# Recurrent heads: the keys and queries of a head in three tiles of memory, one for each chunk of tokens, in place of one

## The chip, the cores and the metric

The kernel runs on one core of a Trainium2 chip, in one launch. The metric is the device time of one execution in microseconds (us). The core's engines are TensorE (PE in the profile: matrix products; PEld are its weight loads, which run beside the products), VectorE (DVE), ScalarE (ACT), GpSimd (POOL) and SyncE (SP, which here only issues DMA transfers). Each engine works through its own queue in the order in which the program was written; between engines, semaphores make an instruction wait for another engine's.

## The reference

Two layers of a transformer trunk over 128 context tokens and 1024 latent tokens, D_MODEL = 1024. Layer 0 is attention beside a short convolution, layer 1 a gated linear recurrence (HGRN2) that runs over the tokens in both directions; each is followed by a gated feed-forward part with a convolution. The change is in layer 1:

```python
def decay(f_raw, lb_d):
    f = lb_d + (1.0 - lb_d) * jax.nn.sigmoid(f_raw)
    return heads(jnp.log(f)), heads(1.0 - f)          # log decay, key
...
b = jnp.cumsum(gb, axis=2)
o_inter = jnp.einsum('bhtk,bhkv->bhtv', qb * jnp.exp(b), S)
decay = jnp.exp(jnp.where(lower, diff, -jnp.inf))      # diff: b[t] - b[s]
scores = jnp.einsum('bhtk,bhsk,bhtsk->bhts', qb, kb, decay)
o = o_inter + jnp.einsum('bhts,bhsv->bhtv', scores, vb)
```

There are 8 heads with 128 key and 128 value channels, and each is scanned forward and backward.

## The kernel before

All 1152 tokens are handled as 9 tiles of 128 tokens, and these as three **chunks** c of 384 tokens, taken in the order 2, 1, 0. In the recurrent layer the head's arrays lie with the 128 key channels on the partitions and tokens along the free dimension. `X` is one tile `[128, 4, 1152]` with four arrays: KBF (forward keys), QAB (queries for the backward scan), QAF (queries for the forward scan) and KBB (backward keys). The same memory is used by all eight heads.

In place of a scan over tokens, the scores are built by doubling: for each of seven **levels** (half-block length 1, 2, ... 64) and each chunk there is one **item**, 21 items in a head, in the order level 0 with chunks 2, 1, 0, then level 1, and so on. An item consists of

- `mixed_keys` (L1610): ACT copies keys of both directions, interleaved in runs of the half-block length, from KBF and KBB of the chunk into a scratch tile `km` (L1613). It is written one item ahead: the copy of item n+1 stands ahead of item n's own work;
- `level` (L1616): three products on TensorE with interleaved queries of the chunk from QAB and QAF (L1624; each appears as two records in the trace), then two **updates** in place that multiply half the columns of the chunk by decays: POOL does arrays 0 and 1, DVE arrays 2 and 3 (both L1630), and a predicated copy on DVE takes the scores out of PSUM (L1632);
- `fill`: TensorE goes on with a few **steps** of the projections of the next head (one step is three products of 384 columns into `psp`, L93 to L95). The number of steps after an item is the number left for the head, spread evenly. The last head (h = 7) has only two projections left to do.

After the items of a head, `flip` and `states` make the states at the tile bounds, `output` reads QAB, QAF and the states, and meanwhile `arrays` writes the next head's X, chunk by chunk (KBF and KBB by ACT at L1583, QAF by POOL at L1584, QAB by DVE at L1585). `diagonal` (L1602) ends on ACT with a copy of TensorE's products (L1608), right ahead of the first `km` copy of the head.

The order on every engine is the order of the code. The waits between engines are set by the build: an instruction that reads or writes part of a tile waits for earlier ones that touch the same stretch of that tile, from the first address to the last. For the interleaved read of two arrays it is these lines that give the addresses; the pattern goes from the first array to the second and back for each run of h elements:

```python
base = X[:, a0, c0:c0 + n]
return bass.AP(base.tensor, base.offset,
               [list(base.ap[0]), [2 * h, n // (2 * h)], [(a1 - a0) * NTOK + h, 2], [1, h]])
```

Of the kernel before, what the change touches and what calls it, by code (L numbers as in the profile page):

```python
# [12 lines left out]
I32 = mybir.dt.int32  # L13
AF = mybir.ActivationFunctionType
ALU = mybir.AluOpType
# [5 lines left out]
P = 128  # L21
# [3 lines left out]
NTOK = 1152  # L25
# [55 lines left out]
def build(tc, ins, outs, consts):  # L81
    nc = tc.nc
    ctx = ExitStack()
    mm = nc.tensor.matmul
# [41 lines left out]
    ident = cst.tile([P, P], F32, name="ident")  # L126
# [218 lines left out]
    def bank(name):  # L345
        return pd.tile([P, 512], F32, tag="d", name=name)

    with ExitStack() as st:
# [16 lines left out]
        ps = bank("psA")  # L365
# [86 lines left out]
        ps = bank("psB")  # L452
        nc.tensor.transpose(ps[:, 0:P], rB, ident)
        nc.vector.tensor_copy(colB, ps[:, 0:P])
        ps = bank("psC")
# [32 lines left out]
    def feature(pu, col, n_in, col0):  # L488

        w = wload(wcols(w_in, col), KT, P)  # L490
        ps = pu.tile([P, 3, 512], F32, tag="u", name="psu")
        for c in (2, 1, 0):
            a = col0 + c * OW
            for k in range(KT):
                mm3(ps[:, c, :n_in], (w[0][:, k, :], w[1][:, k, :]),
                    (hT[0].k(k, a, n_in), hT[1].k(k, a, n_in)), k == 0, k == KT - 1)
        return ps

    with ExitStack() as st:
# [46 lines left out]
        for j in (4, 5, 0, 1, 2, 3):  # L546
            ps = psk if j == 4 else feature(pus[(j + 1) % 2], j * P, OW, 1)
# [6 lines left out]
            for c in (2, 1, 0):  # L554
# [4 lines left out]
                if keys and j != 4:  # L559
                    n, k2 = keys.pop(0)  # L560
                    put_keys(n, k2.rearrange("p (h d) -> p h d", d=HD))
                t0, n, off = (1, 2, P) if c == 0 else (3 * c, 3, 0)
# [53 lines left out]
    with ExitStack() as st:  # L616
# [4 lines left out]
        for j in range(4):  # L621
            cw = [colB[:, 96 + 4 * t + j:97 + 4 * t + j] for t in range(3)]
            ps = feature(pu, 1280 + j * P, IW, 0)
# [4 lines left out]
            ps = feature(pu, 1792 + j * P, IW, 0)  # L628
# [7 lines left out]
            if j < 3:  # L636
                mod_chunk(*mod_todo.pop(0), pd, "d")
            ps = feature(pu, 768 + j * P, OW, 1)
            nc.vector.tensor_tensor(sc32[:, j, :].rearrange("p (a b) -> p a b", b=OW), ps[:, :, :OW], yv,  # L639
                                    op=ALU.mult)  # L640
# [6 lines left out]
    with ExitStack() as st:  # L647
# [109 lines left out]
        def flip(i):  # L757
            g, kt = steps[i]
            pt = bank("ppp")
            for hh in range(4):  # L760
                nc.tensor.transpose(pt[:, hh * P:(hh + 1) * P], Pss[g][hh][:, kt * P:(kt + 1) * P], ident)
            pts[i] = pt
# [70 lines left out]
        with tc.manual_schedule(engines={ET.PE, ET.Activation}):  # L833
# [3 lines left out]
            for i in range(-LEAD - 3, total + PVL):  # L837
                p = i + LEAD
# [23 lines left out]
        for a, b in ((768, SW), (384, 768), (0, 384)):  # L862
            for j in range(4):
# [3 lines left out]
                                                                  op=ALU.subtract)  # L867
# [597 lines left out]
    def first_split(n):  # L1465
# [10 lines left out]
    gp = gpx.enter_context(tc.tile_pool(name="gp", reuse_waits="tile", bufs=1))  # L1476
# [2 lines left out]
    pp = psx.enter_context(tc.tile_pool(name="ppG", reuse_waits="tile", bufs=2, space=PSUM))  # L1479
    psc = psx.enter_context(tc.tile_pool(name="pscG", reuse_waits="tile", bufs=4, space=PSUM))  # L1480
    masks = gs.tile([P, 7, P], U8, name="masks")
    m32 = gp.tile([P, 4, NTOK], I32, tag="X", name="m32").rearrange("p a b -> p (a b)")[:, :7 * P].rearrange(
        "p (a b) -> p a b", b=P)
    nc.sync.dma_start(m32, consts["masks"])
    ng = colB[:, 108:109]
# [1 line left out]
    shared = {}  # L1487

    def persistent(name, shape):

        if name not in shared:
            shared[name] = gp.tile(shape, F32, tag=name, name=name)
        return shared[name]
# [11 lines left out]
    def pmt():  # L1505
        return pm.tile([P, 512], F32, tag="m", name="psm")

    def pst():
        return psc.tile([P, 512], F32, tag="s", name="pss")

    def wtile(name):
        return gp.tile([P, 384], F32, tag="w", bufs=8, name=name)

    KBF, QAB, QAF, KBB = range(4)

    def scan_ap(X, a0, a1, c0, n, h):

        base = X[:, a0, c0:c0 + n]
        return bass.AP(base.tensor, base.offset,
                       [list(base.ap[0]), [2 * h, n // (2 * h)], [(a1 - a0) * NTOK + h, 2], [1, h]])  # L1520

    def colsof(c):
        return slice(c * 384, (c + 1) * 384)

    def t3(ap):
        return ap.rearrange("p (a b) -> p a b", b=P)

    class Head:
# [40 lines left out]


        def begin(self):
            self.X = persistent("X", [P, 4, NTOK])
            self.sT = persistent("sT", [P, NT, P])
            self.T128 = gp.tile([P, 2, NT], F32, tag="T128", bufs=2, name="T128")
            self.tots = {}
# [3 lines left out]
            nc.sync.dma_start(self.S0, ins["state_hgrn"][0, 0, :, self.h].rearrange("r k v -> k r v"))  # L1579

        def arrays(self, c):
            X, fb, q, cols = self.X, self.fb, self.q[c], colsof(c)
            nc.scalar.activation(X[:, 0:4:3, cols], fb[:, :, cols], AF.Identity, bias=one, scale=-1.0)  # L1583
            nc.gpsimd.tensor_tensor(X[:, QAF, cols], q, fb[:, 0, cols], op=ALU.mult)  # L1584
            nc.vector.tensor_tensor(X[:, QAB, cols], q, fb[:, 1, cols], op=ALU.mult)  # L1585
            kk = self.kk[c] = wtile("kk")
            nc.vector.tensor_tensor(kk, X[:, KBF, cols], X[:, KBB, cols], op=ALU.add)

        def totals(self, c):

# [19 lines left out]
        def mixed_keys(self, lv, c):  # L1610
            km = self.km[lv, c] = wtile("km")
            hh = 1 << lv
            nc.scalar.copy(km.rearrange("p (n s r) -> p n s r", s=2, r=hh),  # L1613
                           scan_ap(self.X, KBF, KBB, c * 384, 384, hh))

        def level(self, lv, c):  # L1616
            X, cols = self.X, colsof(c)
            hh = 1 << lv
            nb = 192 // hh
            ps = pst()  # L1620
            km = self.km.pop((lv, c))
            for q3 in range(3):
                c0 = c * 384 + q3 * P
                mm(ps[:, q3 * P:(q3 + 1) * P], km[:, q3 * P:(q3 + 1) * P], scan_ap(X, QAB, QAF, c0, P, hh),  # L1624
                   start=True, stop=True)
            t4 = self.tots[c][lv].rearrange("p a (n s) -> p a n s", s=2)
            for half, arrs in ((0, slice(0, 2)), (1, slice(2, 4))):
                x = X[:, arrs, cols].rearrange("p a (n s r) -> p a n s r", s=2, r=hh)[:, :, :, half, :]
                eng = nc.vector if half else nc.gpsimd
                eng.tensor_tensor(x, x, t4[:, :, :, 1 - half].unsqueeze(3).to_broadcast([P, 2, nb, hh]),  # L1630
                                  op=ALU.mult)
            nc.vector.copy_predicated(self.sT[:, 3 * c:3 * c + 3, :],  # L1632
                                      masks[:, lv:lv + 1, :].to_broadcast([P, 3, P]), t3(ps[:, :384]))


        def state_at(self, dr, t):
            if t == (8 if dr else 1):
                return self.S0[:, dr, :]
            return self.X[:, KBB if dr else KBF, t * P:(t + 1) * P]

        def flip(self, dr, c):
            pt = pmt()
            for q3 in range(3):
                t = 3 * c + q3
                nc.tensor.transpose(pt[:, q3 * P:(q3 + 1) * P],
                                    self.X[:, KBB if dr else KBF, t * P:(t + 1) * P], ident)
            kb = wtile("kb")
            nc.scalar.activation(kb, pt[:, :384], AF.Copy)
            return kb
# [18 lines left out]

        def output(self, c):
            po = pst()  # L1670
            X, V = self.X, shared["V"]
            for q3 in range(3):
                t = 3 * c + q3
                cols = slice(t * P, (t + 1) * P)
                o = po[:, q3 * P:(q3 + 1) * P]
                mm(o, self.sT[:, t, :], V[:, t, :], start=True, stop=t == 0)
                if t:
                    mm(o, X[:, QAB, cols], self.state_at(1, t), start=False, stop=False)
                    mm(o, X[:, QAF, cols], self.state_at(0, t), start=False, stop=True)
            self.done.add(c)  # L1680
            sq = wtile("sq")
            ss = gp.tile([P, 4], F32, tag="ss", bufs=2, name="ss")
            nc.scalar.activation(sq, po[:, :384], AF.Square)
            nc.vector.tensor_reduce(ss[:, :3], t3(sq), axis=AX.X, op=ALU.add)
            nc.vector.tensor_scalar(ss[:, :3], ss[:, :3], 1.0 / P, EPS, op0=ALU.mult, op1=ALU.add)
            nc.gpsimd.tensor_tensor(ss[:, :3], ss[:, :3], mhalf[:, 0:3], op=ALU.pow)
            on = wtile("on")
            nc.vector.tensor_tensor(t3(on), t3(po[:, :384]), ss[:, :3].unsqueeze(2).to_broadcast([P, 3, P]),
                                    op=ALU.mult)
            return on  # L1690
# [128 lines left out]
    one = gp.tile([P, 1], F32, name="one")  # L1819
# [294 lines left out]
```

## Time and profile before

| | us |
|---|---|
| median of 3 runs (3276.28 to 3280.92) | 3277.81 |
| profiled execution | 3279.65 |
| its span, first to last instruction | 3277.9 |
| TensorE busy | 3144.1 (96%) |
| TensorE weight loads busy | 2910.5 (89%) |
| DVE busy | 2248.1 (69%) |
| POOL busy | 1421.4 (43%) |
| ACT busy | 1289.4 (39%) |

The profiled execution's time is its span and 1.75 us around it. The items of the eight heads run from about 1594 to 2323 us of the span. The page's table by 40 slices shows where each engine is busy; a TensorE that is busy nearly all the time is not one that loses nothing, since its records overlap each other (a product of 384 columns is recorded as 0.34 us, and the next one starts 0.17 us after it). What is lost shows in the idle time ahead of a product or a weight load, and in the distance from start to start.

### The profile page before, as it was taken

What the parts mean: (1) busy time and instruction counts of PE and PEld (TensorE: products, weight loads), DVE (VectorE), ACT (ScalarE), POOL (GpSimd) and SP (SyncE); (2) the same over time, 40 slices, a digit from 0 to 9 for tenths busy, and PEclk for the clock granted to TensorE, in tenths of its full rate; (3) what the DMA queues carried; (4) which work ended last, traced back from release to release, by engine and by line L of the source; (5) the groups of instructions that cost most, each with busy time, mean ns of one, the idle gap of its engine ahead of it and who ended that gap; (6) DMA issues with size and microseconds to landing.
All of it is one profiled execution on the core that took longest, in us unless ns stands there. A gap on an engine that the chain in (4) does not pass through costs nothing. (4 is left out here: it accounts for less than half of the span.)

```text
span 3277.9 us, 48732 instructions
## 1 busy us (share of the span) xinstructions
PE 3144.1 (96%) x19231; PEld 2910.5 (89%) x19231; DVE 2248.1 (69%) x3117; ACT 1289.4 (39%) x2162; POOL 1421.4 (43%) x1007
## 2 busy tenths in 40 slices
PE   7989999899999998998999999999999999998997
PEld 6989888789999997877999999999779999997886
DVE  6778888548988875674466666655556888774356
ACT  4311998333333333115433334343444333334112
POOL 6821332335545534562244343333425554443565
PEclk9999999999999999999999999999999999999999
DMA  7152000322322326541222222211331323225452
GB/s 220 35 136 90 1 1 8 129 84 68 96 92 86 89 82 210 175 153 64 95 85 75 64 68 81 59 56 37 117 116 53 100 77 97 74 68 181 150 170 84
DMA packets 267476, 305.42 MB, mean 93 GB/s; under 512 B 19587, under 2 KB 200015, under 8 KB 267248
## 3 DMA queue, kind: packets, MB, share of 16 engines
q1 hardware_dynamic: 266448, 300.67, 29.0%
q8 instruction: 152, 2.49, 0.3%
q0 software_dynamic: 800, 1.63, 0.2%
q14 instruction: 76, 0.62, 0.1%
HBM read 237.84 MB, written 64.42 MB: 92 GB/s over the span
## 5 line engine op out<-in xcount | busy, mean ns | idle before, releaser
L1098 POOL TENSOR_TENSOR wlo<-S,whi 128x512 fp32r<-128x512 f32 x152 | 245.0, 1626 | 250.8 <-ACT whi L1097 249.5
L93 PE MATMUL psd<-whi,s 128*128 128x512 f32 x720 | 286.1, 397 | 18.0 <-ACT y L1347 17.0
L109 POOL TENSOR_TENSOR wlo<-wraw,whi 128x1024 fp32r<-128x1024 f32 x78 | 196.3, 2520 | 232.5 <-ACT whi L108 221.7
L94 PE MATMUL psd<-wlo,s 128*128 128x512 f32 x720 | 285.1, 396 | 0.0
L95 PE MATMUL psd<-whi,s 128*128 128x512 f32 x720 | 285.0, 396 | 0.0
L1630 POOL TENSOR_TENSOR X<-X,tot 128x384 f32<-128x384 f32 x144 | 181.0, 1257 | 228.4 <-PE pss L1624 175.6
L1126 DVE SCALAR_TENSOR_TENSOR t<-u,fcw,t 128x1156 f32<-128x1156 f32 x152 | 262.8, 1747 | 13.5 <-ACT t L1121 10.8
L95 PE MATMUL psq<-T,wlo 128*128 128x290 f32 x912 | 270.8, 297 | 0.0
L94 PE MATMUL psq<-T,whi 128*128 128x290 f32 x912 | 270.3, 296 | 0.0
L93 PE MATMUL psq<-T,whi 128*128 128x290 f32 x912 | 270.1, 296 | 0.0
L1098 POOL TENSOR_TENSOR wlo<-wraw,whi 128x512 fp32r<-128x512 f32 x114 | 182.6, 1603 | 172.3 <-ACT whi L1097 156.6
L108 ACT ACTIVATE whi<-wraw 128x1024 fp32r<-128x1024 f32 x130 | 136.7, 1054 | 289.8 <-DMA wraw<-in_ffn_w_down_dram 120.9
L1097 ACT ACTIVATE whi<-S 128x512 fp32r<-128x512 f32 x152 | 92.9, 628 | 323.1 <-DVE S L1076 247.3
L1349 DVE TENSOR_TENSOR y<-y,psd 128x512 f32<-128x512 f32 x144 | 98.0, 684 | 170.9 <-PE psd L95 170.4
L213 DVE SCALAR_TENSOR_TENSOR macc<-mraw,sil,macc 128x512 f32<-128x512 f32 x182 | 192.1, 1095 | 7.3 <-DMA mraw<-in_w_mod_dram 7.3
L93 PE MATMUL psu<-h,whi 128*128 128x388 f32 (+1 forms) x504 | 175.0, 348 | 12.7 <-DVE sc L639 7.3
L93 PEld LDWEIGHTS psd<-whi,s 128*128 128x128 f32 x720 | 136.1, 189 | 52.3 <-ACT y L1347 19.5
L1630 DVE TENSOR_TENSOR X<-X,tot 128x384 f32<-128x384 f32 x144 | 102.5, 712 | 114.1 <-PE pss L1624 76.5
L1624 PE MATMUL pss<-X,km 128*128 128x128 f32 x1008 | 153.0, 289 | 24.3 <-POOL X L1630 10.4
L94 PE MATMUL psu<-h,whi 128*128 128x388 f32 (+1 forms) x504 | 174.4, 346 | 1.9 <-POOL h L428 1.9
L93 PE MATMUL psp<-s,whi 128*128 128x384 f32 x480 | 174.8, 364 | 0.0
L95 PE MATMUL psu<-h,wlo 128*128 128x388 f32 (+1 forms) x504 | 173.2, 344 | 0.0
(438 smaller groups left out, 10046.7 us busy)
## 6 DMA issues: line engine op xcount, KB each, us to landing
wraw<-in_ffn_w_up_dram SPq DMA_DIRECT2D x88, 512.0 KB, 3.8
mraw<-in_w_mod_dram SPq DMA_DIRECT2D x104, 256.0 KB, 2.8
sraw<-sd SPq DMA_DIRECT2D x44, 578.0 KB, 4.6
wraw<-in_ffn_w_down_dram SPq DMA_DIRECT2D x44, 512.0 KB, 4.0
sd<-t SPq DMA_DIRECT2D x38, 578.0 KB, 3.1
wraw<-in_hgrn_w_in_dram SPq DMA_DIRECT2D x40, 512.0 KB, 4.0
mraw<-in_w_mod_dram SPq DMA_DIRECT2D x28, 512.0 KB, 3.9
wraw<-in_attn_w_in_dram SPq DMA_DIRECT2D x18, 512.0 KB, 4.4
```

The source lines that it names most:

```text
L93: mm(ps, l[0], r[0], start=start, stop=False)
L94: mm(ps, l[0], r[1], start=False, stop=False)
L95: mm(ps, l[1], r[0], start=False, stop=stop)
L108: nc.scalar.activation(hi[:, :n], raw[:, :n], AF.Copy)
L109: (eng or nc.gpsimd).tensor_tensor(lo[:, :n], raw[:, :n], r32(hi[:, :n]), op=ALU.subtract)
L213: nc.vector.scalar_tensor_tensor(acc[:, cond, :], raw, sil[:, cond, k:k + 1], acc[:, cond, :], op0=ALU.mult, op1=ALU.add)
L1097: nc.scalar.activation(hi, src, AF.Copy)
L1098: nc.gpsimd.tensor_tensor(lo, src, r32(hi), op=ALU.subtract)
L1126: nc.vector.scalar_tensor_tensor(t, u[:, :, c0:c0 + HO], taps(p + NF * x)[c0], t, op0=ALU.mult, op1=ALU.add)
L1349: nc.vector.tensor_tensor(y[t][:, cols], y[t][:, cols], ps, op=ALU.add)
L1624: mm(ps[:, q3 * P:(q3 + 1) * P], km[:, q3 * P:(q3 + 1) * P], scan_ap(X, QAB, QAF, c0, P, hh), start=True, stop=True)
L1630: eng.tensor_tensor(x, x, t4[:, :, :, 1 - half].unsqueeze(3).to_broadcast([P, 2, nb, hh]), op=ALU.mult)
```

## The change

`X` becomes a list of three tiles `[128, 4, 384]`, one for each chunk; all that read or wrote a stretch of columns of the one tile now use the chunk's tile. The distance between two arrays goes from 1152 to 384 elements. No instruction is added, taken away or moved on any engine.

```diff
-    m32 = gp.tile([P, 4, NTOK], I32, tag="X", name="m32").rearrange("p a b -> p (a b)")[:, :7 * P].rearrange(
+    m32 = gp.tile([P, 4, 384], I32, tag="X0", name="m32").rearrange("p a b -> p (a b)")[:, :7 * P].rearrange(
...
-                       [list(base.ap[0]), [2 * h, n // (2 * h)], [(a1 - a0) * NTOK + h, 2], [1, h]])
+                       [list(base.ap[0]), [2 * h, n // (2 * h)], [(a1 - a0) * 384 + h, 2], [1, h]])
...
-            self.X = persistent("X", [P, 4, NTOK])
+            self.X = [persistent(f"X{c}", [P, 4, 384]) for c in range(3)]
...
-            X, fb, q, cols = self.X, self.fb, self.q[c], colsof(c)
-            nc.scalar.activation(X[:, 0:4:3, cols], fb[:, :, cols], AF.Identity, bias=one, scale=-1.0)
-            nc.gpsimd.tensor_tensor(X[:, QAF, cols], q, fb[:, 0, cols], op=ALU.mult)
-            nc.vector.tensor_tensor(X[:, QAB, cols], q, fb[:, 1, cols], op=ALU.mult)
+            X, fb, q, cols = self.X[c], self.fb, self.q[c], colsof(c)
+            nc.scalar.activation(X[:, 0:4:3, :], fb[:, :, cols], AF.Identity, bias=one, scale=-1.0)
+            nc.gpsimd.tensor_tensor(X[:, QAF, :], q, fb[:, 0, cols], op=ALU.mult)
+            nc.vector.tensor_tensor(X[:, QAB, :], q, fb[:, 1, cols], op=ALU.mult)
...
-                           scan_ap(self.X, KBF, KBB, c * 384, 384, hh))
+                           scan_ap(self.X[c], KBF, KBB, 0, 384, hh))
...
-            X, cols = self.X, colsof(c)
+            X = self.X[c]
...
-                c0 = c * 384 + q3 * P
-                mm(ps[:, q3 * P:(q3 + 1) * P], km[:, q3 * P:(q3 + 1) * P], scan_ap(X, QAB, QAF, c0, P, hh),
+                mm(ps[:, q3 * P:(q3 + 1) * P], km[:, q3 * P:(q3 + 1) * P], scan_ap(X, QAB, QAF, q3 * P, P, hh),
                    start=True, stop=True)
...
-                x = X[:, arrs, cols].rearrange("p a (n s r) -> p a n s r", s=2, r=hh)[:, :, :, half, :]
+                x = X[:, arrs, :].rearrange("p a (n s r) -> p a n s r", s=2, r=hh)[:, :, :, half, :]
```

`state_at`, `flip` and `output` take the chunk's tile in the same way.

In the listings below, a row is one instruction in the order of its engine, with the engines whose semaphore it waits for; X_14569 is the tile of chunk 2, X_14568 that of chunk 1 and X_14567 that of chunk 0. First ACT in head 0, from the copy that ends `diagonal` on, before:

```order
L1608 ACTIVATE sT<-pss 128x384 [waits PE_49] x2
L1613 COPY km<-X 128x384 [waits DVE_49,Activation_49,Pool_49]
L1613 COPY km<-X 128x384
L1566 ACT_TABLE_LOAD
L1566 ACTIVATE sg<-psp 128x384 [waits PE_49]
L1613 COPY km<-X 128x384 [waits DVE_49,Pool_49] x2
```

and after:

```order
L1608 ACTIVATE sT<-pss 128x384 [waits PE_49] x2
L1613 COPY km<-X_14569 128x384 [waits DVE_49,Pool_49]
L1613 COPY km<-X_14568 128x384 [waits DVE_49,Pool_49]
L1566 ACT_TABLE_LOAD
L1566 ACTIVATE sg<-psp 128x384 [waits PE_49]
L1613 COPY km<-X_14567 128x384 [waits DVE_49,Activation_49,Pool_49]
```

Nothing moved. Each copy now names the tile of its own chunk, and its wait is for the engines that wrote that tile last.

Next TensorE in head 7, at level 1 of chunks 1 and 0, with one step of projections between them, before:

```order
L95 MATMUL psp<-h_13782,wlo 128x384
L1624 MATMUL pss<-X,km 128x128 [waits Pool_49]
L1624 MATMUL pss<-X,km 128x128 x2
L93 MATMUL psp<-h_13782,whi 128x384
L94 MATMUL psp<-h_13783,whi 128x384
L95 MATMUL psp<-h_13782,wlo 128x384
L1624 MATMUL pss<-X,km 128x128 [waits Pool_49]
L1624 MATMUL pss<-X,km 128x128 x2
```

and after:

```order
L95 MATMUL psp<-h_13782,wlo 128x384
L1623 MATMUL pss<-X_14568,km 128x128 [waits Activation_49]
L1623 MATMUL pss<-X_14568,km 128x128 x2
L93 MATMUL psp<-h_13782,whi 128x384
L94 MATMUL psp<-h_13783,whi 128x384
L95 MATMUL psp<-h_13782,wlo 128x384
L1623 MATMUL pss<-X_14567,km 128x128 [waits Activation_49]
L1623 MATMUL pss<-X_14567,km 128x128 x2
```

Again nothing moved. An item's first product waited for POOL, and now waits for ACT, which makes `km`. In the changed program this is so in all 21 items of the head; before, 12 of the 21 waited for POOL or DVE.

Last POOL, the updates of head 7 from its first item on, before:

```order
L1630 TENSOR_TENSOR X<-X,fb 128x2x192 [waits DVE_49,PE_49,Activation_49]
L1630 TENSOR_TENSOR X<-X,fb 128x2x192 [waits PE_49,Activation_49] x2
L1630 TENSOR_TENSOR X<-X,tot 128x2x96x2 [waits PE_49,Activation_49] x3
L1630 TENSOR_TENSOR X<-X,tot 128x2x48x4 [waits PE_49,Activation_49] x3
L1630 TENSOR_TENSOR X<-X,tot 128x2x24x8 [waits PE_49,Activation_49] x3
```

and after:

```order
L1629 TENSOR_TENSOR X_14569<-X_14569,fb 128x384 [waits PE_49,Activation_49]
L1629 TENSOR_TENSOR X_14568<-X_14568,fb 128x384 [waits PE_49,Activation_49]
L1629 TENSOR_TENSOR X_14567<-X_14567,fb 128x384 [waits DVE_49,PE_49,Activation_49]
L1629 TENSOR_TENSOR X_14569<-X_14569,tot 128x192x2 [waits PE_49,Activation_49]
L1629 TENSOR_TENSOR X_14568<-X_14568,tot 128x192x2 [waits PE_49,Activation_49]
```

The order is the same. The operand that is written has one dimension less, since the two arrays now follow each other without a gap; the number of elements, the runs and the step between them are as they were. The engines named are the same too, but the copy on ACT that the update waits for is now the one of its own chunk, which is an item older.

## Rows read from the trace of the kernel before

**Rows 1.** Busy time by stretch: PE, PEld, DVE, ACT, POOL; clock, DMA share, GB/s.

```profile
1599.00:1606.00 7.00, 5.31 (x23) 4.99 (x22) 3.21 (x7) 1.26 (x2) 3.11 (x2) 0.76 0.00 0
...
1685.00:1780.00 95.00, 93.03 (x618) 91.71 (x617) 63.95 (x112) 37.09 (x66) 40.72 (x30) 1.00 0.26 81
...
2280.00:2322.00 42.00, 32.34 (x208) 28.55 (x209) 27.91 (x50) 16.75 (x29) 25.85 (x20) 1.00 0.26 80
...
2322.00:2350.00 28.00, 26.54 (x164) 22.83 (x164) 13.85 (x27) 14.27 (x25) 7.92 (x8) 1.00 0.46 153
```

**Rows 2.** Waits, 1590 to 2360 us: total us, times, longest.

```profile
POOL X L1630 <- ACT km L1613: 67.1, 41, 3.5
...
PEld pss L1624 <- POOL X L1630: 15.5, 16, 2.0
...
PEld pss L1624 <- ACT km L1613: 12.8, 11, 1.3
...
PEld pss L1624 <- DVE X L1630: 5.8, 10, 0.8
```

**Rows 3.** Waits of the weight loads, 1590 to 1685 us (head 0).

```profile
PEld pss L1624 <- POOL X L1630: 3.6, 4, 2.0
```

**Rows 4.** Waits of the weight loads, 2275 to 2325 us (head 7).

```profile
PEld pss L1624 <- POOL X L1630: 8.5, 6, 1.6
PEld pss L1624 <- ACT km L1613: 3.4, 4, 1.3
PEld pss L1624 <- issue: 1.3, 1, 1.3
PEld pss L1624 <- DVE X L1630: 0.8, 1, 0.8
```

**Rows 5.** Timeline, head 0's first item: start, length, engine, [idle before <- releaser].

```profile
1593.24 0.49 ACT L1608 ACTIVATE sT<-pss 128x384 f32<-128x384 f32 x1 [1.22 <-PE pss L1606]
...
1593.62 1.25 ACT L1613 COPY km<-X 128x384 f32<-128x384 f32 x2
1594.35 0.95 PEld L1624 LDWEIGHTS pss<-X,km 128*128 128x128 f32 x6 [1.34 <-ACT km L1613]
```

**Rows 6.** Timeline, head 0's third item.

```profile
1600.41 1.55 POOL L1630 TENSOR_TENSOR X<-X,fb 128x384 f32<-128x384 f32 x1 [3.49 <-ACT km L1613]
...
1602.02 1.43 PE L1624 MATMUL pss<-X,km 128*128 128x128 f32 x6 [1.69 <-POOL X L1630]
```

**Rows 7.** Timeline, head 7's first two items of level 2.

```profile
2295.65 0.83 PE L1624 MATMUL pss<-X,km 128*128 128x128 f32 x6
...
2296.23 0.42 PE L93 MATMUL psp<-s,whi 128*128 128x384 f32 x1
...
2296.67 0.34 PE L95 MATMUL psp<-s,wlo 128*128 128x384 f32 x1
...
2296.94 1.28 POOL L1630 TENSOR_TENSOR X<-X,tot 128x384 f32<-128x384 f32 x1 [0.62 <-ACT km L1613]
...
2298.27 0.75 PEld L1624 LDWEIGHTS pss<-X,km 128*128 128x128 f32 x6 [1.59 <-POOL X L1630]
2298.27 0.94 PE L1624 MATMUL pss<-X,km 128*128 128x128 f32 x6 [1.26 <-POOL X L1630]
...
2298.96 0.42 PE L93 MATMUL psp<-s,whi 128*128 128x384 f32 x1
```

**Rows 8.** Timeline, head 7 at level 0: updates of its first two items.

```profile
2281.89 1.17 POOL L1630 TENSOR_TENSOR X<-X,fb 128x384 f32<-128x384 f32 x1 [5.78 <-PE pss L1624]
2282.01 1.46 DVE L1630 TENSOR_TENSOR X<-X,fb 128x384 f32<-128x384 f32 x1
...
2283.11 1.25 PE L1624 MATMUL pss<-X,km 128*128 128x128 f32 x6 [0.84 <-POOL X L1630]
...
2284.47 0.56 DVE L1630 TENSOR_TENSOR X<-X,fb 128x384 f32<-128x384 f32 x1 [0.47 <-PE pss L1624]
2284.51 1.55 POOL L1630 TENSOR_TENSOR X<-X,fb 128x384 f32<-128x384 f32 x1 [1.45 <-PE pss L1624]
```

More of the change, by code (lines that the diff above doesn't have):

```diff
@@ L1581, in arrays @@
         def arrays(self, c):
-            X, fb, q, cols = self.X, self.fb, self.q[c], colsof(c)
-            nc.scalar.activation(X[:, 0:4:3, cols], fb[:, :, cols], AF.Identity, bias=one, scale=-1.0)
-            nc.gpsimd.tensor_tensor(X[:, QAF, cols], q, fb[:, 0, cols], op=ALU.mult)
-            nc.vector.tensor_tensor(X[:, QAB, cols], q, fb[:, 1, cols], op=ALU.mult)
+            X, fb, q, cols = self.X[c], self.fb, self.q[c], colsof(c)
+            nc.scalar.activation(X[:, 0:4:3, :], fb[:, :, cols], AF.Identity, bias=one, scale=-1.0)
+            nc.gpsimd.tensor_tensor(X[:, QAF, :], q, fb[:, 0, cols], op=ALU.mult)
+            nc.vector.tensor_tensor(X[:, QAB, :], q, fb[:, 1, cols], op=ALU.mult)
             kk = self.kk[c] = wtile("kk")
-            nc.vector.tensor_tensor(kk, X[:, KBF, cols], X[:, KBB, cols], op=ALU.add)
+            nc.vector.tensor_tensor(kk, X[:, KBF, :], X[:, KBB, :], op=ALU.add)
         def totals(self, c):
@@ L1638, in state_at @@
                 return self.S0[:, dr, :]
-            return self.X[:, KBB if dr else KBF, t * P:(t + 1) * P]
+            return self.X[t // 3][:, KBB if dr else KBF, t % 3 * P:(t % 3 + 1) * P]
         def flip(self, dr, c):
@@ L1643, in flip @@
             for q3 in range(3):
-                t = 3 * c + q3
                 nc.tensor.transpose(pt[:, q3 * P:(q3 + 1) * P],
-                                    self.X[:, KBB if dr else KBF, t * P:(t + 1) * P], ident)
+                                    self.X[c][:, KBB if dr else KBF, q3 * P:(q3 + 1) * P], ident)
             kb = wtile("kb")
@@ L1670, in output @@
             po = pst()
-            X, V = self.X, shared["V"]
+            X, V = self.X[c], shared["V"]
             for q3 in range(3):
                 t = 3 * c + q3
-                cols = slice(t * P, (t + 1) * P)
+                cols = slice(q3 * P, (q3 + 1) * P)
                 o = po[:, q3 * P:(q3 + 1) * P]
```

## The prediction

> **What bounds the kernel now.** I read the busy times by stretch first. In a head in the middle (1685 to 1780 us) TensorE is busy 93.0 of 95 us, DVE 64.0, POOL 40.7, ACT 37.1 [rows 1]: TensorE sets the pace and has almost no gaps. In the items of the last head (2280 to 2322) it is busy only 32.3 of 42, and its weight loads 28.6; DVE is busy 27.9, POOL 25.9 and ACT 16.8 [rows 1]. No engine is full there, so a chain of waits sets the pace. That is because this head has few projection steps to put between its items.
>
> Next the waits, by who waited for whom. POOL's updates waited 41 times for a `km` copy on ACT, 67.1 us in all [rows 2]. By the code an update of item n reads or writes nothing that the copy for item n+1 touches, since that copy belongs to another chunk; it waits because both lie in the stretch of the one tile X between first and last address. The same holds for the copy of item n+1 behind the updates of item n-1, and for the products of item n behind those updates. So there is a ring over all three chunks: update, copy for the item after next, update, copy. The timeline of head 7 shows it: POOL's update at 2296.94 was let go by ACT's copy, and the next products at 2298.27 by POOL [rows 7].
>
> What the ring costs is read from TensorE's own waits at L1624. Its weight loads waited 15.5 us for POOL's update, 5.8 for DVE's and 12.8 for ACT's copy [rows 2], and 1.3 us with no releaser named [rows 4]: 35.4 us in the stage. All else in the kernel is left as it is.
>
> **The change, part by part.**
>
> *The first item of each head: nothing.* The first `km` copy stands in ACT's queue right behind the copy that ends `diagonal`, and that one waits for TensorE's last products of the head before. TensorE then waits 1.34 us for these two ACT instructions [rows 5]. The false wait on the arrays of chunk 0 goes, but the queue stays, so 8 x 1.34 = 10.7 us stay. That leaves 35.4 - 10.7 = 24.7 us: 3.6 in head 0 [rows 3], in head 7 8.5 + 0.8 + 1.3 + (3.4 - 1.34) = 12.7 [rows 4], and 24.7 - 3.6 - 12.7 = 8.4 in heads 1 to 6, or 1.4 each.
>
> *The waits for POOL and DVE go whole.* Where products waited for the update of another chunk, their own `km` was ready long before, because that update had itself been held until that copy was done (at 2296.94 POOL starts as the copy ends, and TensorE waits until POOL is done 1.28 us later [rows 7]). So nothing else is late right behind this wait. What is late next is the chunk's own chain: products of 0.58 us or more [rows 7], an update of at most 1.55 [rows 8], a copy of some 0.62 (two in 1.25 [rows 5]), about 3 us. It has three items' time. By the code heads 0 to 6 have some four steps (twelve products, 0.17 us apart) behind an item, so an item is at least 0.58 + 2.0 = 2.6 us, and three are 7.8: covered.
>
> *What a wait is worth.* A wait of a weight load is not quite time lost. In the second item of rows 7 the step before started its last product at 2296.67; the next would start 0.17 us later, an item without a wait takes 2296.23 - 2295.65 = 0.58, so the next step was due at 2297.42 and came at 2298.96: 1.54 lost, where the weight load shows 1.59 and the product 1.26 [rows 7]. Other waits are nearer to the product's figure, so I take 0.9 of the weight loads' time: 24.7 x 0.9 = 22.2 us. The ends are 0.8 (1.26 / 1.59), 19.8 us, and 1.0, 24.7 us.
>
> The Trainium skill (Perfetto Trace Analysis, Identifying the Most-Contended Engine) says that the busy share of matmuls is a bad measure, since pipelined ones overlap in the trace, and that of weight loads a good one. By products, head 7 idles 42 - 32.3 = 9.7 us, by weight loads 42 - 28.6 = 13.4; the start-to-start reading above sides with the loads, as that page would have it.
>
> *The clock in head 0.* Between 1599 and 1606 us the granted clock was 0.76 on average [rows 1], behind the longest wait of the stage (product idle for 1.69 us, POOL held by ACT for 3.49 before it [rows 6]). 7 x (1 - 0.76) = 1.7 us is the most that it can have cost; part of it was waiting anyway. With the wait gone the fall should go: 1.3 us, between 0 and 1.7.
>
> *What takes the ring's place in head 7.* Without it 42 - 0.9 x 12.7 = 30.6 us would be left for TensorE, just above DVE's 27.9 and POOL's 25.9 [rows 1]. ACT still has weight splits, loads of a function table and evacuations between its copies, and with 1.5 us for an item they will make TensorE wait here and there. The waits for ACT and without a releaser, 1.3 + 2.1 = 3.4 us [rows 4], are the upper end of what stays, 0 the lower; I take 2.5, so that head 7 gives 9 of its 11.4.
>
> *Costs that the trace does not show.* The updates write through one dimension less; runs and elements are the same. POOL's lie between 1.17 and 1.55 us at level 0, DVE's between 0.56 and 1.46 [rows 8], and I take no change. Up to (33 - 25.9) / 21 = 0.34 us more per POOL update would be hidden in head 7, and far more elsewhere. TensorE and ACT read X in runs that jump between two arrays: the jump is now 384 elements and not 1152, the runs are as long as before. I take no change; the bounds are in the last rival. At the start of the stage the first writes of the three tiles wait for what lay in this memory before at other instructions than the one tile's did; nothing there is on the path, as TensorE's projections queued there need none of X.
>
> *Sum.* 22.2 + 1.3 - 2.5 = 21.0 us; rounded down to 20 for small waits that stay. The profiled execution (3279.65, of which the span is 3277.9) would become 3259.7; the median before is 1.84 us below it, so the forecast for the median is 3277.8 - 20 = **3258 us**.
>
> **The rivals.**
>
> *Given back behind head 7.* The stage after the items needs transposes, states, and loaded heads and weights by DMA. If these do not come sooner, head 7's 9 us are waited for there: 20 - 9 = 11 us, 3267. For it: the DMA share is 0.46 from 2322 to 2350. Against: TensorE is busy 26.5 of those 28 us [rows 1], and those transfers are issued when TensorE, ACT or DVE release their buffers, so they move along.
>
> *DVE loses the race for its second input.* In head 7's first item POOL started 0.12 us ahead and DVE's update took 1.46 us; in the second DVE started first, took 0.56, and POOL took 1.55 [rows 8]. With POOL released earlier, and DVE held in its queue by other work, more DVE updates may fall behind: 0.9 us each. With all 21 of head 7 behind, DVE has 27.9 + 18.9 = 46.8 us where the stretch had 42: 5 us lost there in place of 9 won. Elsewhere 64.0 + 18.9 = 82.9 of 95 us stay hidden. That makes 20 - 9 - 5 = 6 us, 3272. It begins to count from (33 - 27.9) / 0.9 = 6 of the 21 on. The Trainium skill (SBUF — State Buffer, Who interferes with whom) has this as a lock: a DVE instruction with two inputs in SBUF and a GpSimd one that reads SBUF exclude each other, and who starts first keeps it to the end. The first two items agree with it.
>
> *It does nothing.* If the copies themselves were what is late, TensorE would wait for ACT as long as it did for POOL: 3277. Against it: an update held by a copy ends over a microsecond after that copy [rows 7].
>
> *Slower: the interleaved read.* The six records of an item take 1.25 us at level 0 [rows 8] and, also behind a wait, 0.94 at level 2 [rows 7]: 0.31 us for shorter runs. If the nearer jump brought this price to all levels, the 6 x 24 = 144 items of levels 1 to 6 would cost 44.6 us more, on the engine that is the bound: 3258 + 44.6 = 3303. It cancels the gain at 20 / 144 = 0.14 us an item. At the other end the 24 items of level 0 would lose their surcharge, a gain of 7.4 us. For either speaks only that no row has this distance; against, that the price goes with the length of runs, which stays.
>
> **How the numbers follow.** Forecast 0.70, between 3252 (24.7 + 1.3 us saved) and 3265; given back 0.10 at 3267; DVE behind POOL 0.09 at 3272; nothing 0.05 at 3277; slower 0.06. A measurement of this kernel tells 0.2% (6.6 us) from no change. Faster by more than that: 0.70 + 0.10 = 0.80; within it: 0.09 + 0.05 = 0.14; slower: 0.06. The range goes from 3252 to 3272, which leaves out the last two cases and the tails.
>
> **What would show it.** TensorE's waits at the products are left with ACT alone, near 8 x 1.34 = 10.7 us and 1 to 4 more in head 7; POOL and DVE are gone as releasers. POOL's updates no longer wait for ACT. Head 7's 42 us become about 33, heads 1 to 6 lose 1.4 us each. The granted clock in head 0's items stays at 1.00. An item of level 2 without a wait still takes 0.58 us from start to start; if it takes more, the last rival is at work, and if DVE's updates rise well above 0.6 us, the second. If the items are shorter but the end is not, the time was given back behind 2322 us.

## The result and the profile after

| | before | after |
|---|---|---|
| median of 4 runs each, us | 3277.88 | 3259.15 |
| lowest to highest | 3276.28 to 3280.92 | 3256.95 to 3259.99 |
| span of the profiled execution | 3277.9 | 3257.8 |
| TensorE busy in it | 3144.1 (96%) | 3136.7 (96%) |
| DVE busy | 2248.1 (69%) | 2257.3 (69%) |

The ratio of the times is 0.9939, with a 95% interval from 0.9927 to 0.9951: faster, by 18.7 us where 20 were forecast. The busy share of TensorE says nothing of it: 96% before and after.

In the changed kernel L1624 has become L1623 (the products of an item) and L1630 has become L1629 (its updates). The waits of the weight loads from 1590 to 2345 us (engine, tile and line, releaser: total us, times, longest), the answer to [rows 2], are all of them these:

```profile
PEld pss L1623 <- ACT km L1613: 15.0, 14, 1.3
PEld psm L1643 <- ACT V L1561: 3.5, 7, 0.5
PEld pse L93 <- ACT y L1792: 3.1, 4, 2.0
PEld pse L94 <- DVE wlo L109: 0.2, 1, 0.2
```

POOL and DVE are gone as releasers of an item's products. Of the 15.0 us, 8 x 1.34 = 10.7 are the first items; 4.3 are left in head 7. From the waits of all engines in the same stretch, what POOL's updates and ACT's copies wait for now:

```profile
POOL X L1629 <- PE pss L1623: 269.5, 141, 18.6
...
POOL X L1629 <- ACT km L1613: 15.2, 8, 2.5
...
ACT km L1613 <- DVE X L1629: 13.0, 8, 2.9
...
ACT km L1613 <- POOL X L1629: 3.0, 3, 1.2
```

An update now waits for the products of its own item, 141 times, as it has to. It was held by a copy 41 times for 67.1 us [rows 2]; 8 of these rows are left. 7 of them, at the third item of head 0 and the second of heads 1 to 6, are updates ahead of which a copy and the last product end less than 0.1 us from each other.

Where the time went is read best from stretches cut at the first product of head 0, head 1, head 2, and at head 7's first product and its last. Length, then busy time of PE, PEld, DVE, ACT and POOL, the clock, DMA share and GB/s, before:

```profile
1594.30:1690.20 95.90, 92.38 (x606) 90.56 (x606) 63.42 (x123) 36.42 (x66) 41.06 (x31) 0.98 0.19 58
1690.20:1788.70 98.50, 96.53 (x643) 95.21 (x643) 66.10 (x120) 38.80 (x70) 41.73 (x31) 1.00 0.26 82
2280.50:2321.80 41.30, 32.13 (x206) 28.35 (x207) 27.28 (x47) 16.25 (x28) 25.65 (x20) 1.00 0.26 81
```

and after:

```profile
1592.20:1683.20 91.00, 89.85 (x607) 89.44 (x607) 65.51 (x122) 35.74 (x66) 40.81 (x31) 1.00 0.20 62
1683.20:1780.60 97.40, 96.00 (x643) 95.34 (x643) 66.80 (x120) 38.05 (x70) 40.50 (x31) 1.00 0.26 82
...
2265.90:2299.00 33.10, 30.64 (x206) 28.66 (x207) 31.06 (x47) 15.85 (x28) 23.13 (x20) 1.00 0.32 101
```

Head 0 takes 4.9 us less. Heads 1 to 6 together went from 590.3 to 582.7 us, 7.6 less. Head 7, from its first product to the first `flip` behind its items, went from 42.8 to 34.7, 8.1 less. That is 20.6 us. The stage also began 2.1 us earlier in this execution, and 2.6 us were lost again behind it, which makes the 20.1 between the two spans. In the profile of the second run of the change (below) the same three lengths are 4.9, 7.6 and 9.0 us less than before, and again 2.6 are lost behind.

The last row holds something that was only a rival in the prediction. In head 7 DVE is now busy 31.1 of 33.1 us, where it was 27.3 of 41.3, with the same 47 instructions. By form, DVE's updates at 2280 to 2322 us before (xcount | busy us, mean ns | idle before):

```profile
L1630 DVE TENSOR_TENSOR X<-X,tot 128x384 f32<-128x384 f32 x17 | 10.6, 624 | 10.5 <-ACT km L1613 5.4 <-PE pss L1624 5.1
...
L1630 DVE TENSOR_TENSOR X<-X,fb 128x384 f32<-128x384 f32 x3 | 2.6, 860 | 2.4 <-PE pss L1624 2.4
```

and at 2262.5 to 2300 us after:

```profile
L1629 DVE TENSOR_TENSOR X<-X,tot 128x384 f32<-128x384 f32 x17 | 13.6, 802 | 1.7 <-PE pss L1623 1.3
...
L1629 DVE TENSOR_TENSOR X<-X,fb 128x384 f32<-128x384 f32 x3 | 3.7, 1235 | 0.0
L109 DVE TENSOR_TENSOR wlo<-wraw,whi 128x1024 fp32r<-128x1024 f32 x2 | 3.7, 1842 | 0.0
```

The same 20 updates take 17.3 us in place of 13.2, and no longer find DVE idle. What that does to TensorE is in the timeline of head 7 after the change (start, length, engine, [idle before <- releaser]):

```profile
2273.93 1.82 DVE L109 TENSOR_TENSOR wlo<-wraw,whi 128x1024 fp32r<-128x1024 f32 x1
...
2275.39 1.25 POOL L1629 TENSOR_TENSOR X<-X,tot 128x384 f32<-128x384 f32 x1 [0.72 <-PE pss L1623]
...
2275.68 1.38 DVE L1629 TENSOR_TENSOR X<-X,tot 128x384 f32<-128x384 f32 x1
...
2276.13 0.83 PE L1623 MATMUL pss<-X,km 128*128 128x128 f32 x6
...
2276.71 0.42 PE L93 MATMUL psp<-s,whi 128*128 128x384 f32 x1
...
2277.15 0.51 ACT L1613 COPY km<-X 128x384 f32<-128x384 f32 x1 [2.54 <-DVE X L1629]
...
2277.71 0.74 PEld L1623 LDWEIGHTS pss<-X,km 128*128 128x128 f32 x6 [0.55 <-ACT km L1613]
```

DVE splits a weight tile until 2275.75. Its update, delayed by that, begins behind POOL's, runs 1.38 us, and ACT makes the copy for the next item of that chunk only then; TensorE waits 0.55 us. This is a true chain, one chunk's own. The item at 2276.13, without a wait, still takes 2276.71 - 2276.13 = 0.58 us.

DVE is behind only a part of the 4.3 us that are left in head 7. Three of the six waits, 0.55, 0.23 and 0.69 us, follow copies that waited for DVE's updates: 1.5 us. The other three, 0.53, 1.03 and 1.27 us, follow copies that waited for no engine but stood in ACT's queue behind its other work: 2.8 us. For the 0.53 and the 1.27 this work ends with a weight split (L108); for the 1.03 it is a table load and an evacuation, which had themselves come late, behind a copy that waited for DVE. The first and the last of the three in the timeline after:

```profile
2272.69 1.05 ACT L108 ACTIVATE whi<-wraw 128x1024 fp32r<-128x1024 f32 x1
...
2273.64 0.96 ACT L1613 COPY km<-X 128x384 f32<-128x384 f32 x2
...
2274.24 0.79 PEld L1623 LDWEIGHTS pss<-X,km 128*128 128x128 f32 x6 [0.53 <-ACT km L1613]
...
2293.65 0.74 PEld L1623 LDWEIGHTS pss<-X,km 128*128 128x128 f32 x6 [1.27 <-ACT km L1613]
```

### The profile page after: what moved, and what is told of

It is laid out like the page before. It is cut to its first block, busy times and chain, and to the rows that moved or that the text cites. A ratio compares the mean times of both kernels' runs of the same rounds, so it can differ in the third digit from the quotient of the medians.

```text
span 3257.8 us, 48737 instructions
## 1 busy us (share of the span) xinstructions
PE 3136.7 (96%) x19231; PEld 2913.3 (89%) x19231; DVE 2257.3 (69%) x3117; ACT 1283.7 (39%) x2162; POOL 1409.6 (43%) x1007
## 3 DMA queue, kind: packets, MB, share of 16 engines
q8 instruction: 152, 2.49, 0.3%
## 5 line engine op out<-in xcount | busy, mean ns | idle before, releaser
L1629 POOL TENSOR_TENSOR X<-X,tot 128x384 f32<-128x384 f32 x144 | 170.5, 1184 | 224.1 <-PE pss L1623 208.6
L108 ACT ACTIVATE whi<-wraw 128x1024 fp32r<-128x1024 f32 x130 | 136.6, 1053 | 281.3 <-DMA wraw<-in_ffn_w_down_dram 114.1
L93 PE MATMUL psu<-h,whi 128*128 128x388 f32 (+1 forms) x504 | 175.0, 348 | 11.4 <-DVE sc L639 7.3
L94 PEld LDWEIGHTS psq<-T,whi 128*128 128x128 f32 x912 | 172.7, 189 | 0.0
L95 PEld LDWEIGHTS psq<-T,wlo 128*128 128x128 f32 x912 | 172.6, 189 | 0.0
```

The lines of the kernel that those rows point to most:

```text
L93: mm(ps, l[0], r[0], start=start, stop=False)
L94: mm(ps, l[0], r[1], start=False, stop=False)
L95: mm(ps, l[1], r[0], start=False, stop=stop)
L108: nc.scalar.activation(hi[:, :n], raw[:, :n], AF.Copy)
```

## The experiments

Each run is compared with the kernel before on the same chip: 3277.36 us there for the first four, 3277.59 for the others.

**The change again.** As a measure for the others.

> The changed kernel once more, beside the others of this call. Both theories: about 3259 us, and in the items TensorE waits for ACT's copies alone.

Measured: 3259.82 us, ratio 0.9944 [0.9928, 0.9961]. Weight loads wait 14.3 us for `km`, for POOL and DVE not at all. Head 7's items take 32.3 us, from first to last product.

**One tile, laid out by chunk.** Is it the number of tiles, or the stretch of addresses that one instruction spans?

```diff
...
-            self.X = [persistent(f"X{c}", [P, 4, 384]) for c in range(3)]
+            X = persistent("X", [P, 3, 4, 384])
+            self.X = [X[:, c] for c in range(3)]
```

> One tile again, but laid out chunk by chunk ([128, 3, 4, 384]), so that the stretches of two chunks do not overlap. Theory (a wait is set when two instructions' stretches of addresses overlap): the same waits as with three tiles, so about 3259 us, 19 less than before. Rival (it is the number of tiles, each of which is waited for as a whole): the ring is back, about 3278 us.

Measured: 3259.31 us, 0.9943 [0.9928, 0.9958]. The waits of its weight loads at the items, whole:

```profile
PEld pss L1624 <- ACT km L1614: 14.2, 14, 1.3
```

So the number of tiles is nothing. Laying the four arrays of a chunk side by side, so that an instruction of one chunk ends before another chunk begins, is all of the change.

**Two tiles.** Chunks 0 and 1 share one tile with array distance 768; chunk 2 has its own.

```diff
...
-                       [list(base.ap[0]), [2 * h, n // (2 * h)], [(a1 - a0) * 384 + h, 2], [1, h]])
+                       [list(base.ap[0]), [2 * h, n // (2 * h)], [(a1 - a0) * X.ap[1][0] + h, 2], [1, h]])
...
-            self.X = [persistent(f"X{c}", [P, 4, 384]) for c in range(3)]
+            X01, X2 = persistent("X01", [P, 4, 768]), persistent("X2", [P, 4, 384])
+            self.X = [X01[:, :, 0:384], X01[:, :, 384:768], X2]
```

> Chunk 2 has a tile of its own, chunks 0 and 1 share one, with the arrays over both chunks as before. Theory (the ring over the chunks costs the time): chunk 0's products wait for chunk 1's updates again, chunk 2 is free of both, so about half of the gain is left: head 7's items take about 36 us (41 before, 33 with three tiles), heads 1 to 6 keep most of theirs, in all 3263 to 3269 us. Rival (shorter distance or simpler operands make the instructions faster): chunk 2's instructions alone gain, a third of 19 us, so about 3272 us, and updates or products of chunk 2 are shorter than those of chunks 0 and 1.

Measured: 3267.07 us, 0.9966 [0.9953, 0.9979]: 10.3 us of the gain, a little over half. Weight loads at the items:

```profile
PEld pss L1624 <- ACT km L1614: 11.4, 9, 1.3
PEld pss L1624 <- POOL X L1630: 9.6, 11, 2.3
...
PEld pss L1624 <- issue: 1.3, 1, 1.3
```

POOL's row comes back with 9.6 us. The waits other than the first items' are 9.6 + 1.3 + 0.7 = 11.6 us, where they were 24.7 before and about 4 after; head 7's items take 37.2 us, between 41.3 and 33.1. In that figure there is also a fall of the clock, to 0.79 over 8 us, which can have cost 1.7. Heads 1 to 6, at the full clock in all these profiles, take 4.3 us less than before, where the change gained 7.6. So the gain goes with the false waits. The rival, that chunk 2's instructions are faster, doesn't show: products without a wait take 0.58 to 0.59 us (medians of the levels from 2 on) in each of the three chunks.

**Head 7 without POOL's updates.** What do they cost DVE? The kernel leaves out POOL's half of the updates in head 7, 21 instructions.

```diff
+                if self.h == 7 and not half:
+                    continue
                 eng = nc.vector if half else nc.gpsimd
```

> Three tiles; head 7 leaves out POOL's updates (21 instructions), all else is there. Theory (in head 7 DVE is now held up by POOL, which gets first to what they share): DVE's updates in head 7 fall from a mean of 0.87 us to about 0.56, DVE's busy time from 35 to about 28 us, TensorE's waits for copies from 5.6 to 1.3 to 2.5 us, and the items from 33.1 to about 30.5 us: 2.5 us off the whole. Rival (DVE's updates are long for a reason of their own, their operands' new form): DVE's updates stay near 0.87 us, and the time within 1 us of the three tiles'.

Measured: 3255.33 us, 0.9933 [0.9918, 0.9948], 4.5 below the change. DVE's updates by form from 2263 to 2298 us (here they stand at L1631), and the stretch from the first to the last product of head 7:

```profile
L1631 DVE TENSOR_TENSOR X<-X,tot 128x384 f32<-128x384 f32 x18 | 10.0, 555 | 3.8 <-PE pss L1623 2.8
...
L1631 DVE TENSOR_TENSOR X<-X,fb 128x384 f32<-128x384 f32 x3 | 1.7, 556 | 0.7 <-PE pss L1623 0.7
```

```profile
2266.40:2297.30 30.90, 29.74 (x206) 28.88 (x207) 25.52 (x49) 15.85 (x28) 0.00 (x0) 1.00 0.32 102
```

Without POOL beside it every update on DVE takes 0.56 us, and DVE is busy 25.5 us in place of 31.1. TensorE's items take 30.9 us, 1.4 less than the 32.3 of the change on the same chip. So the races that DVE loses against POOL cost at most 1.4 us of TensorE's time; at most, since this run also takes away POOL as an engine that copies wait for. TensorE's weight loads wait 3.1 us for `km` in head 7, where they waited 4.9 in the change on the same chip: none waits behind DVE any more. Beside the first item's 1.34, waits of 0.54 and 1.27 us are left, both behind a weight split on ACT. The other 3 us of the 4.5 do not lie in these items. In the two profiles the part behind them is 2.4 us shorter; Between them and 2600 us TensorE's clock fell once in this run's profile and three times in that of the change. Why is not shown.

**The first copy of a head, moved ahead.** The first item's wait was left by the change, and is an order of ACT's queue. Here the first `km` copy is written ahead of the last chunk's `diagonal`; all else is the change. In the head loop:

```diff
             nh.diagonal(1)
+            nh.mixed_keys(0, 2)
...
-        hd.mixed_keys(*items[0])
         for n, e in enumerate(items):
```

and the same in the prologue of head 0.

> Three tiles, and the first km copy of each head is written ahead of the last chunk's diagonal, behind the middle one's. Theory (the first item waits only because ACT's queue holds the copy behind the copy that ends diagonal): TensorE's weight loads lose their wait of 1.34 us at the first item of all 8 heads; at 0.9 that is 9.6 us, so about 3250 us. Rival (the copy is late by itself, since the chunk's arrays are written late): the waits move with it, and the time stays within 2 us of 3259.

Measured: 3247.07 us, 0.9908 [0.9894, 0.9921], 12 us below the change. In the profiles heads 0 to 6 together, from head 0's first product to head 7's, are 9.9 us shorter than with the change. The stage begins 1.4 us sooner, which may be head 0's own first item, but its start differs by 2 us between two runs of the change too. Head 7 is 0.8 us longer. The part behind the stage is 3.6 us shorter, with fewer falls of the clock (shown below, under what was given back behind head 7), so not all of the 12 us are the move's. Timeline at the start of head 2:

```profile
1772.56 0.70 ACT L1613 COPY km<-X 128x384 f32<-128x384 f32 x1 [0.81 <-DMA ogd<-og]
...
1775.71 0.83 PE L1606 MATMUL pss<-q,kk 128*128 128x128 f32 x6
...
1776.38 1.15 PE L1623 MATMUL pss<-X,km 128*128 128x128 f32 x6
...
1776.58 0.49 ACT L1608 ACTIVATE sT<-pss 128x384 f32<-128x384 f32 x1 [2.54 <-PE pss L1606]
```

The first product of the head now follows the products of `diagonal` with no wait, ahead of the ACT copy that it used to stand behind; a head's period fell from 97.4 to 96.0 us. Weight loads wait for `km` only in head 7:

```profile
PEld pss L1623 <- ACT km L1613: 5.2, 7, 1.7
```

The longest of these, 1.7 us, is new: it follows a copy that waited for DVE. So head 7 itself gains nothing by the move.

**The same move in the kernel before.** If the two waits were independent, the move would be worth as much here.

> The same move in the kernel before, with one tile. The copy then waits for the arrays of chunk 0 too, which share its stretch of addresses, but these are written before the last diagonal. Theory (the queue alone makes the first item wait): the same 9 to 10 us less, about 3268 us, with the waits for POOL and DVE as they were. Rival (with one tile the early copy waits in ACT's queue and holds up what stands behind it): 3274 us or more.

Measured: 3275.36 us, 0.9991 [0.9983, 1.0]: 2 us, not 10. The waits from 1585 to 2315 us:

```profile
PEld pss L1624 <- POOL X L1630: 20.0, 23, 3.3
PEld pss L1624 <- DVE X L1630: 7.4, 11, 0.8
...
PEld pss L1624 <- ACT km L1613: 2.1, 3, 0.7
PEld pss L1624 <- issue: 1.3, 1, 1.3
```

ACT's row falls from 12.8 to 2.1, and POOL's and DVE's together rise from 21.3 to 27.4: 6.1 of 10.7 come back as ring waits. The timeline in head 2, one head of eight, shows how:

```profile
1785.05 1.16 PE L1624 MATMUL pss<-X,km 128*128 128x128 f32 x6
1785.24 0.49 ACT L1608 ACTIVATE sT<-pss 128x384 f32<-128x384 f32 x1 [1.21 <-PE pss L1606]
...
1785.63 0.68 ACT L1613 COPY km<-X 128x384 f32<-128x384 f32 x1
...
1786.39 1.24 POOL L1630 TENSOR_TENSOR X<-X,fb 128x384 f32<-128x384 f32 x1 [4.42 <-ACT km L1613]
...
1791.80 0.94 PEld L1624 LDWEIGHTS pss<-X,km 128*128 128x128 f32 x6 [0.41 <-POOL X L1630]
```

The first products start early, but POOL's update of that item waits for the second item's copy, another chunk's, which stands behind `diagonal`'s copy in ACT's queue. The second item's update waits for the third's copy in the same way, until 1790.17, and the third item's products then wait for POOL. The second cause is the clock. In head 0 it was 0.72 over 12 us (1596 to 1608), and in head 7's items (2273.0 to 2316.7 us) it was 0.92:

```profile
2273.00:2316.70 43.70, 33.99 (x209) 30.20 (x207) 29.13 (x52) 16.68 (x29) 25.69 (x20) 0.92 0.24 74
```

43.7 x 0.08 = 3.5 us, more than the 2.4 by which these items are longer than the 41.3 of before. That the number of 3268 failed has thus two reasons in the trace. In heads 1 to 6 the clock is full in all four kernels, with and without the move, and there the ring's part can be read: the move gains 4.7 us with one tile (590.3 to 585.6) and 8.5 with the change (582.7 to 574.2). In heads 0 and 7, where the clock fell, this run is 0.9 and 2.4 us longer than before. What the ring and the clock each have in these can't be told apart; the 6.1 us of waits that came back are shown, and that the clock falls because of them is not.

**Weight splits of head 7 on POOL.** The chain shown in head 7 goes through a weight split on DVE. Here the change is kept, and that split goes to POOL (which is what no engine named means in that function).

```diff
-        wts[n] = wsplit(*raws.pop(n), eng=nc.vector)
+        wts[n] = wsplit(*raws.pop(n), eng=nc.vector if n < NS else None)
```

> Three tiles; the weight splits of the output projection in head 7 (128x1024, 1.2 us alone on DVE, 2.5 on POOL) go from DVE to POOL. Theory (in head 7 DVE is the full engine, 35 of 37.5 us, and its late updates hold the copies): DVE's load there falls by 3 to 4 us, TensorE's waits for copies in head 7 fall from 4.3 us beyond the first to 2 to 3, 1 to 2 us off the whole, 3257 to 3258. Rival (POOL's updates now stand behind a split of 2.5 us, and the copies wait for POOL in place of DVE): as much waiting or more, 3259 to 3262.

Measured: 3260.34 us, 0.9946 [0.9934, 0.9959]: no gain. By form, 2263 to 2302 us:

```profile
L109 POOL TENSOR_TENSOR wlo<-wraw,whi 128x1024 fp32r<-128x1024 f32 x2 | 5.0, 2488 | 1.7 <-ACT whi L108 1.7
```

```profile
L1629 DVE TENSOR_TENSOR X<-X,tot 128x384 f32<-128x384 f32 x18 | 16.8, 934 | 2.3 <-PE pss L1623 1.8
```

DVE is rid of two splits, 3.7 us, but its updates rise from 802 to 934 ns with POOL working more beside it, which takes back 18 x 0.13 = 2.4 us; and POOL pays 5.0. TensorE's weight loads in head 7 wait 5.8 us for `km`, no less than the 4.9 to 5.6 of the change: copies that had waited for DVE now wait for POOL, as the rival said.

**Both together.** The early copy and the splits on POOL.

> Three tiles, first copies early and the splits on POOL. The two moves touch different waits, so their effects should add: about 3248 us if both theories hold, 3250 to 3252 if the splits gain nothing.

Measured: 3249.49 us, 0.9915 [0.9901, 0.9928]: the early copy's gain, and nothing from the splits.

## Why the prediction was right, point by point

- **The ring was the cause.** Shown: it goes with the layout alone (one tile by chunk), and half of it with two tiles. TensorE's waits for POOL and DVE, 21.3 us [rows 2], are gone.
- **First items, nothing.** Right: 15.0 us of waits stay, of which 10.7 are these. That the order of ACT's queue is their cause was argued in the prediction, and is shown by the early copy: the wait is gone at every head's first item, and heads 0 to 6 are 9.9 us shorter.
- **0.9 of a weight load's wait is lost time.** Right in heads 1 to 6: forecast 8.4 x 0.9 = 7.6, measured 7.6, and 7.6 and 7.8 in the second run and in one tile by chunk. It is no general price: the early copy took away 6 x 1.34 = 8.0 us of waits there and brought 8.5. The busy share of TensorE showed none of this.
- **Head 0 with its clock.** Forecast 3.6 x 0.9 + 1.3 = 4.5, measured 4.9; the clock over the head went from 0.98 to 1.00.
- **Head 7.** Forecast 9 of 11.4, measured 8.1 in this execution and 9.0 both in the second run of the change and in one tile by chunk. So the term "what takes the ring's place", 2.5 us, came out at 3.3 and 2.4, within what one execution differs from another; by the waits of the weight loads it is 4.3 and 3.6, above the upper end of 3.4. The reason given, ACT's other work, was right for the larger part: 2.8 of the 4.3 us stand behind it. What the reason left out is DVE, 1.5 us: it is nearly full, because its updates are dearer. The row that said so stood in the prediction [rows 8], under a rival with a chance of 0.09, as a matter of all 21 updates or none. It came in part: 4.1 us more DVE time, about five updates of the 0.9 us dearer kind, which cost TensorE at most 1.4 us by the run without POOL's updates. So it cost a little before the rival's point of decision, six, was reached.
- **Given back behind head 7.** A little of it: 2.6 us were lost again, in the profiles of the change, of its second run and of one tile by chunk alike. It is not the DMAs that were feared. Behind head 7 the clock falls at several places. Two of them, where it falls in most of these profiles, differ between them, right after TensorE has waited: 1.56 us with transposes for DVE at the first, 1.5 us with projections for a weight split on ACT at the second. These waits are as long before as after. Stretches of 20 us around the two, before:

```profile
2440.00:2460.00 20.00, 16.79 (x80) 14.83 (x79) 11.88 (x26) 10.72 (x14) 6.92 (x6) 0.91 0.27 82
2524.00:2544.00 20.00, 17.58 (x99) 17.02 (x98) 17.13 (x17) 11.55 (x17) 12.69 (x8) 0.91 0.08 30
```

after:

```profile
2420.00:2440.00 20.00, 16.92 (x79) 15.25 (x79) 9.53 (x24) 9.79 (x12) 4.54 (x5) 0.83 0.33 106
2506.00:2526.00 20.00, 17.60 (x95) 17.04 (x94) 17.17 (x14) 11.41 (x17) 16.12 (x10) 0.83 0.00 0
```

and with the early copy:

```profile
2408.00:2428.00 20.00, 16.80 (x83) 15.05 (x82) 10.72 (x25) 9.69 (x12) 5.73 (x6) 0.91 0.28 86
2490.00:2510.00 20.00, 17.59 (x108) 17.02 (x108) 17.12 (x18) 11.44 (x17) 12.02 (x8) 1.00 0.07 30
```

  20 us at 0.91 lose 1.8 to the clock, at 0.83 3.4. The falls would cost 3.6 us before, 6.8 after and 1.8 with the early copy, if no other wait lay beside them; and behind head 7 the change lost 2.6 us against before while the early copy won 0.9. So the sign and most of the size go with the clock. It is not the chance of one execution: in the second run of the change and in one tile by chunk the falls, a third one near 2330 us among them, reckoned in the same way come to the same 6.8 us. (The falls of the last 320 us, which every profile has, are left out: they come to 12.7 us before, 13.7 after and 11.2 with the early copy.) But the run without POOL's updates keeps the chunks apart too, and there only one of these falls is left and 0.2 us were lost. So a layout by chunk doesn't bring the falls by itself. What decides how many there are stays open.
- **The interleaved read.** Dead as a rival: 0.58 us for an item of level 2 as before [rows 7], with the array distance at 384 as at 1152; an item of level 0 without a wait has records of 1.16 us at either distance (with 1152 the one at 1785.05 above, in the early copy with one tile). The read's price goes with the runs.
- **It does nothing; updates with one dimension less.** Neither shows. POOL's updates of the levels from 1 on average 1.17 us in head 7, where they took 1.28 before.

The forecast of 3258 us was 1.15 us off: 0.4 too little in head 0, 0.9 too much in head 7, and differences ahead of and behind the stage that the sum didn't have. That these two, 2.1 us gained and 2.6 lost, nearly cancel is luck. The stage itself, 20.6 us where the sum said 21.0, is not: each of its parts comes out within 1 us.

The Trainium skill (SBUF — State Buffer, Who interferes with whom) has an explanation for DVE's dearer updates, the lock between a DVE instruction with two inputs in SBUF and a GpSimd one that reads SBUF. The run without POOL's updates agrees: 0.56 us each, all 21, where the change had 0.80 and 1.24 on average.

## What to carry to other kernels

Where waits are set by the stretch from first to last address, an instruction with a large stride claims all that lies between. Lay arrays out by the unit that the work goes through (here chunk by chunk), and count the releasers that no data justifies. And where a second wait stands behind the first, removing one alone may bring less: in heads 1 to 6 the early copy was worth 8.5 us after the layout was mended and 4.7 before, and over the whole kernel, where falls of the clock come in, 12 and 2.

## What the runs showed of the hardware that was not expected

An engine can grow dearer by being released: 20 updates on DVE with the same shapes took 13.2 us while the ring held POOL back, 17.3 us once POOL ran freely, and 21 took 11.7 with POOL silent. Moving a split from DVE to POOL did not help either, 2.49 us there for some 1.8 here, and 0.13 us more for each update beside it.

TensorE's granted clock fell in the items of the kernels with the ring, whole or in part (0.76 over 7 us in head 0 before [rows 1]; 0.72 over 12 us in head 0 and 0.92 over 43.7 us in head 7 of the early copy with one tile; 0.79 over 8 us in head 7 with two tiles), at TensorE's longest waits there, of 2.0 to 3.3 us, and in no head's items of the kernels that keep the chunks apart. At equal work behind the stage 20 us with a fall lost 1.8 us in one execution and 3.4 in another, so differences of 2 us in a span are not a mechanism until the clock row has been read.
